# A token mixer rewritten as one software pipeline with a Toeplitz convolution and a list scheduler, on eight Trainium2 cores

## The chip, the cores and the metric

The kernel runs on the eight cores of one Trainium2 chip. Each core works alone on its own half of a stream, and no core talks to another. The metric is the device time of the slowest core in microseconds (us). Executions fall into two states: in the slow one, the cores of one die, sometimes of both, show a lower granted TensorE clock, and the time is longer (in one run of the kernel before, 3508.7 us with the cores of one die at a clock of 0.82, against 3098 us at 0.95). The profile and the trace are of one execution, on its slowest core.

Names used below: TensorE does matrix multiplications ("PE" in the profile, its weight loads "PEld"), VectorE is "DVE", ScalarE "ACT", GpSimd "POOL", SyncE "SP". GpSimd and SyncE issue nearly all DMAs here. PSUM is the memory that the matmuls write, which the kernel uses as eight banks; SBUF holds the other tiles. In the traces here each engine runs its instructions in the order in which the program gives them to it (run e4 shows what that can cost: one wait of 117.8 us). The transfers of one issuing engine keep their order too: of those whose landing the traces before tell (249 of GpSimd, 211 of SyncE), none landed before one that the same engine had issued earlier.

## The reference, cut to what matters

```python
x = x + 0.5 * swiglu_ffn(x, g_ff1, w_ff1_in, w_ff1_out)      # 1024 -> 2 x 2816 -> 1024
z = rms_norm(x, g_mix) @ w_in                                # 1792 columns: conv value, conv gate, q, k, v
u = cv * sigmoid(cg)
c_out = silu(layer_norm(depthwise_causal_conv31(u) + b_dw))  # 512 channels, 31 taps
q, k = rope(rms_norm(q)), rope(rms_norm(k))                  # 8 query heads, 2 key heads of 64
a_out = sink_attend(q, k, v)                                 # own chunk of 64 and the two before it
x = x + concat(c_out, a_out) @ w_out
x = x + 0.5 * swiglu_ffn(x, g_ff2, w_ff2_in, w_ff2_out)
```

A core has 4096 prompt tokens, 128 tokens of history (the halo) and 64 sample tokens. The weights of one SwiGLU are 16.9 MB (22 loads of 512 KB and 22 of 256 KB in the trace), and the program puts the tiles of each stage in the place of those of the stage before. So it has three phases: A (first SwiGLU), the mixer, and C (second SwiGLU). The residual goes through DRAM between phases (`x1`, `x2`).

## The kernel before

Before the change every engine gets its instructions in the order in which the Python program writes them. The mixer takes four tiles of 1024 tokens, one after the other, and in each tile the stages GLU, Q/K, V, conv with attention, output projection follow each other. The conv uses a diagonal weight matrix per tap: 31 matmuls for 128 channels and 256 tokens.

```python
def conv_chunk(sub, c):                 # 128 channels, N = 256 tokens
    yb = nxt("ab") % 2
    for t in range(31):
        O.mm(pb[yb][:, 0:N], DIAG[:, c, t, :], rhs_fn(c, t), t == 0, t == 30)
    ...
def mixer(t):                           # one tile of 1024 tokens
    for i in range(4): ...              # GLU: value and gate projections, sigmoid on ScalarE
    qk_run(chains)                      # Q/K projections, norm, rotation
    ...                                 # V projections
    conv_run(subs, att_tail)            # conv, layer norm; attention is woven in
    ...                                 # attention of the remaining groups
    for (r, n, m0) in ...:              # output projection
        O.dma("sync", "x1%d" % xi, x[0:n, :], d.x1[r:r + n, :], rk=[("x1", r)])
        ...
        O.dma("gpsimd", "x2%d" % xi, d.x2[r:r + n, :], x[0:n, :], wk=[("x2", r)])
...
A.run(loads(A))                         # 22 up-weights, then 22 down-weights, all on the GpSimd queue
mixer_phase(K, base)
Cc.run(loads(Cc))
```

## Time and profile before

The median was 3098.5 us (3096.4 to 3099.8). The trace gives this division on the slowest core (core 5):

| stretch (us) | what | length | TensorE busy |
|---|---|---|---|
| 0 to 1048 | first SwiGLU | 1048 | about 99% from 110 on |
| 1048 to 1128 | border to the mixer | 80 | 7 us |
| 1128 to 2062 | mixer | 934 | 753 us |
| 2062 to 2111 | border to the second SwiGLU | 49 | 4 us |
| 2111 to 3098 | second SwiGLU | 987 | 959 us |

These are the lines of the windows view of the kernel before. Each line has the stretch, its length, then the busy microseconds and the instruction count of PE, PEld, DVE, ACT and POOL, then the granted clock, the share of time in which the 16 DMA engines were busy, and GB/s.

```profile
40.00:110.00 70.00, 67.00 (x365) 34.75 (x363) 21.60 (x59) 18.09 (x31) 13.19 (x25) 1.00 1.04 192
110.00:1000.00 890.00, 881.85 (x5251) 493.61 (x5249) 335.24 (x1030) 225.19 (x388) 35.77 (x67) 0.99 0.19 65
...
1048.00:1128.00 80.00, 7.02 (x43) 5.10 (x43) 11.85 (x35) 5.76 (x8) 12.96 (x24) 0.52 0.72 140
1128.00:2062.00 934.00, 753.11 (x4625) 436.93 (x4624) 421.59 (x992) 463.03 (x1004) 20.34 (x38) 0.91 0.15 45
2062.00:2111.00 49.00, 3.83 (x29) 2.66 (x29) 11.53 (x43) 5.67 (x9) 9.59 (x19) 0.50 0.94 182
```

The SwiGLUs are full: 881.85 of 890 us. In the two borders TensorE does nearly nothing while the DMA engines are busy for 72% and 94% of the time, and in the mixer TensorE is idle for 181 us. The waits view of TensorE in the mixer (microseconds in total, times, longest one) says what ends that idle time:

```profile
PE PS L207 <- DVE B_t L207: 95.2, 64, 3.8
PE PS L207 <- ACT B_t L207: 80.7, 52, 5.0
```

These are 116 short waits for the two engines that finish Q, K, the sigmoid and the softmax: a stage waits for its own chain because no other stage is at hand. The longest piece of the first border is one transfer. In the chain of waits (start, length, what), the load of the sample keys, issued 4 us after the mixer's first weights, takes 35 us:

```profile
1062.07 0.55 SPq L237
1062.66 0.58 SPq L237
1063.35 35.45 DMA B_t<-ck
```

### The profile page before, as it was taken

Reading aid. Unit: us, or ns where it says so; the run is one execution under the profiler, and the core shown is the slowest. Engines: PE = TensorE matmul, PEld = TensorE weight load, DVE = VectorE, ACT = ScalarE, POOL = GpSimd, SP = SyncE. Lnnn points to the kernel's source line nnn. Section 1 sums busy time; section 2 is a strip of 40 time slices with the busy share of each in tenths; the row PEclk is TensorE's granted clock in tenths of the full one; section 3 lists DMA queues with packets and bytes.
Section 4 is the critical chain, followed back from the end, with each engine's and each line's share of the span. In section 5 each row is a group of like instructions: output and inputs, shape, how many; then the busy total and the mean of one; then the engine's idle time right before and its main releaser. Section 6 shows DMA issues by size and latency. Waiting matters only on the chain.

```text
span 3098.4 us, 45235 instructions; the slowest of 8 cores (3075.5 to 3098.4 us)
## 1 busy us (share of the span) xinstructions
PE 2723.2 (88%) x16155; PEld 1537.3 (50%) x16155; DVE 1096.3 (35%) x2948; ACT 915.0 (30%) x1797; POOL 133.7 (4%) x253
## 2 busy tenths in 40 slices
PE   4899999999999546978877887757899999999998
PEld 2455555555555223733633734524455555555554
DVE  3234443333343225344445344423222233332211
ACT  2122222222221114453455545622111122211210
POOL 2100000000000100000000000011000000000000
PEclk9999999999999767989989999887899999999999
DMA  9712111111111430112111130059410111111110
GB/s 199 138 60 72 72 72 48 52 62 62 65 59 52 102 67 7 42 35 70 48 68 42 35 116 1 1 146 193 109 51 32 55 55 55 62 62 62 48 42 21
DMA packets 66731, 204.71 MB, mean 66 GB/s; under 512 B 9452, under 2 KB 11514, under 8 KB 66511
## 3 DMA queue, kind: packets, MB, share of 16 engines
q0 software_dynamic: 33520, 103.14, 13.6%
q1 hardware_dynamic: 32991, 98.68, 10.0%
q8 instruction: 133, 2.18, 0.3%
q14 instruction: 87, 0.71, 0.1%
HBM read 183.67 MB, written 61.39 MB: 79 GB/s over the span
## 4 chain that ended last, share of the span: by engine, by line
PE 75%; DMA 12%; ACT 6%; DVE 3%; issue 3%; POOL 0%; SPq 0%; ACTq 0%; DVEq 0%; POOLq 0%
PE PS L207 75%; ACT B_t L207 6%; DVE B_t L207 3%; DMA C_wd<-wd 2%; DMA A_wu<-wu 2%; DMA C_wu<-wu 2%; DMA A_wd<-wd 2%; DMA B_t<-ck 2%; DMA B_t<-x 1%; DMA x<-B_t 1%; DMA B_t<-sconv 0%; DVE A_sm L207 0%; SPq L237 0%; DMA B_t<-cv 0%; ACTq L179 0%
## 5 line engine op out<-in xcount | busy, mean ns | idle before, releaser
L207 PE MATMUL PS<-B_t 128*128 128x256 bf16 (+5 forms) x4620 | 752.6, 323 | 175.1 <-DVE B_t L207 91.5
L207 PEld LDWEIGHTS PS<-B_t 128*128 128x128 bf16 (+1 forms) x4620 | 436.9, 103 | 490.2 <-issue 294.3
L207 PE MATMUL PS<-A_xnt,A_wu 128*128 128x384 bf16 (+1 forms) x3872 | 650.5, 329 | 3.0 <-DVE A_h L207 2.1
L207 PE MATMUL PS<-C_xnt,C_wu 128*128 128x384 bf16 (+1 forms) x3872 | 631.2, 325 | 6.3 <-DVE C_h L207 3.0
L207 PEld LDWEIGHTS PS<-A_xnt,A_wu 128*128 128x128 bf16 x3872 | 377.0, 98 | 258.9 <-issue 6.1
L207 PEld LDWEIGHTS PS<-C_xnt,C_wu 128*128 128x128 bf16 x3872 | 378.6, 98 | 248.2 <-issue 8.3
L207 PE MATMUL PS<-A_wd,A_h 128*128 128x512 bf16 (+1 forms) x1496 | 330.3, 381 | 7.8 <-DMA A_wd<-wd 7.8
L207 PE MATMUL PS<-C_wd,C_h 128*128 128x512 bf16 (+1 forms) x1452 | 322.3, 383 | 13.2 <-DMA C_wd<-wd 13.2
L207 ACT ACTIVATE C_sa<-PS 128x384 f32<-128x384 f32 (+1 forms) x242 | 117.7, 486 | 721.6 <-PE PS L207 704.8
L207 ACT ACTIVATE B_t<-B_t 128x256 f32<-128x256 f32 (+5 forms) x467 | 235.2, 505 | 131.5 <-DVE B_t L207 92.9
L207 DVE TENSOR_TENSOR C_h<-PS,C_sa 128x384 bf16<-128x384 f32 (+1 forms) x242 | 131.8, 550 | 377.0 <-PE PS L207 376.9
L207 DVE TENSOR_TENSOR A_h<-PS,A_sa 128x384 bf16<-128x384 f32 (+1 forms) x242 | 133.9, 562 | 349.3 <-PE PS L207 349.2
L207 ACT ACTIVATE A_sa<-PS 128x384 f32<-128x384 f32 (+1 forms) x242 | 120.0, 496 | 448.2 <-PE PS L207 432.7
L207 PEld LDWEIGHTS PS<-A_wd,A_h 128*128 128x128 bf16 (+1 forms) x1496 | 146.6, 98 | 183.4 <-issue 13.3
L207 PEld LDWEIGHTS PS<-C_wd,C_h 128*128 128x128 bf16 (+1 forms) x1452 | 143.3, 99 | 189.2 <-issue 23.3
L207 ACT ACTIVATE B_t<-PS 128x512 bf16<-128x512 f32 (+5 forms) x252 | 122.0, 534 | 260.6 <-PE PS L207 260.6
L207 DVE TENSOR_TENSOR B_t<-PS,B_t 128x512 f32<-128x512 f32 (+6 forms) x194 | 120.2, 632 | 212.9 <-ACT B_t L207 131.8
L207 ACT ACTIVATE B_t<-PS,B_t 128x128 f32<-128x128 f32 (+4 forms) x288 | 127.3, 488 | 113.6 <-PE PS L207 109.3
L207 DVE SCALAR_TENSOR_TENSOR C_xr<-PS,C_xr 128x512 f32<-128x512 f32 (+1 forms) x66 | 45.6, 692 | 289.6 <-PE PS L207 289.6
L207 DVE TENSOR_TENSOR B_t<-B_t 128x256 f32<-128x256 f32 (+7 forms) x192 | 100.7, 525 | 53.4 <-ACT B_t L207 45.0
L207 DVE SCALAR_TENSOR_TENSOR A_xr<-PS,A_xr 128x512 f32<-128x512 f32 (+1 forms) x68 | 46.8, 689 | 186.7 <-PE PS L207 186.7
L207 DVE CAST B_t<-B_t 128x256 bf16<-128x256 f32 (+2 forms) x73 | 21.0, 291 | 206.5 <-ACT B_t L207 155.1
(52 smaller groups left out, 1022.3 us busy)
## 6 DMA issues: line engine op xcount, KB each, us to landing
A_xa<-xin SPq DMA_DIRECT2D x33, 512.0 KB, 3.7
A_xr<-xin SPq DMA_DIRECT2D x33, 512.0 KB, 5.6
x<-A_xr POOLq DMA_DIRECT2D x33, 512.0 KB, 3.3
B_t<-x SPq DMA_DIRECT2D x32, 512.0 KB, 6.6
x<-B_t POOLq DMA_DIRECT2D x32, 512.0 KB, 4.0
C_xa<-x SPq DMA_DIRECT2D x32, 512.0 KB, 5.1
C_xr<-x SPq DMA_DIRECT2D x32, 512.0 KB, 7.4
yout<-C_xr POOLq DMA_DIRECT2D x32, 512.0 KB, 2.9
```

The costliest lines, as they stand in the source:

```text
L207: self.P.add(eng, lambda e: getattr(e, meth)(**kw), r, w)
```

## The change

The intent is to keep TensorE busy in the mixer, and to give it less to do there. It has four parts.

1. **Toeplitz conv.** Tokens are permuted so that four phases (token number mod 4) of 32 channels fill 128 partitions. A weight matrix of 128 x 128 then holds four taps for four input and four output phases, and 9 matmuls replace 31: for 128 tokens and 512 channels, 4,608 columns in place of 15,872.
2. **One pipeline** over 32 groups of 128 tokens. Step n projects group n, attends for group n-1, convolves one eighth of a 1024-token tile (from step 10 on), and projects the output of group n-22. There are 10 steps of fill and 12 of drain. Conv inputs and outputs change layout through DRAM (`ud`, `zd`).
3. **A list scheduler** sets the order on every engine, in all three phases. It walks through the operations with a table of modelled costs, and looks ahead by up to 24 units (an operation, or a group of matmuls) on each engine.
4. **Conv weights** of 4.7 MB are made by VectorE in phase A and stored to DRAM, between the up-weights and the down-weights of the first SwiGLU.

Scores and values also use tiles of 64 rows or 64 columns in place of zero-padded full ones. The diff, cut to its core:

```diff
+WINDOW = {"sync": 24, "scalar": 24, "vector": 24, "gpsimd": 24, "tensor": 24}
+    def schedule(self):
+        ...                                   # per engine: first ready unit within WINDOW, else the one ready soonest
+        self.order = [o for u in order for o in units[u]]
-        for t in range(31):
-            O.mm(pb[yb][:, 0:N], DIAG[:, c, t, :], rhs_fn(c, t), t == 0, t == 30)
+        p = self.pb[6][:, half * 256:half * 256 + 256]
+        with self.O.group():
+            for dd in range(9):
+                O.mm(p, self.wr[q][:, half, dd * 128:(dd + 1) * 128], self.US[:, g, dd:dd + N], ..., dd == 8, loose=True)
+    def transp(self, QN, n, dst, q=True):
+        p = self.pb[6][:, 0:5 * n // 2].bitcast(BF16).rearrange("p (j n) -> p j n", j=5)
+        ...                                   # five transposes on TensorE
+        O.cp(dst[:, j0:5, :], p[:, j0:5, :])
+    def run(self, on_step=None):
+        for n in range(last_step):
+            if proj: self.glu_pe(n); self.glu_act(n)
+            if att: self.transp(trq, 128, self.QKT[n % 4])
+            ...                               # statistics, conv, scores, Q/K/V projections, values
+            if og >= 0:
+                for h in range(2):
+                    self.out_pe(r, 128, self.out_lhs(og), h)
-    A.run(loads(A))
-    mixer_phase(K, base)
+    def prologue():
+        step = conv_weights(K, A.wd_off + 15 * 2048)
+        for j in range(NJ):
+            A.load_w(j)
+        for g in range(16):
+            step(g)                           # VectorE makes the weights of 32 channels, GpSimd stores them
+        for j in range(NJ):
+            A.load_d(j)
+    A.run(prologue)
+    M = Mixer(K, base); M.setup(); M.run()
     Cc.run(loads(Cc))
+    P.schedule()
```

## The prediction

> **What bounds the kernel now.** The windows view splits the slowest core's 3098 us into three. First SwiGLU, to 1048 us: after a start of about 40 us TensorE is 99% busy (882 of 890 us between 110 and 1000). Mixer, 1048 to 2062: TensorE is busy 760 of 1014 us. Second SwiGLU, first up-projection at 2111: again 98 to 99%. The chain of waits shows what the rest is: 80 us between 1048 and 1128 (loads of ck and sconv behind 35 us of weights), then in each 1024-token tile about 31 us GLU, 34 us Q/K (TensorE 23 busy, waiting for ScalarE and VectorE), 127 us conv and attention (101 busy), 24 us output projection (x1 loads and x2 stores on the chain); the first tile takes 286 us, not 216. Last, 49 us (2062 to 2111) of waiting for the second SwiGLU's weights and x, and 13 us for its down-weights. Only the mixer and its borders can be won.
>
> **What the change does.** Both SwiGLUs keep their matmuls. In the mixer the 31-tap diagonal conv (31 matmuls of 256 columns per 128 channels and 256 tokens) becomes 9 matmuls for 4 tokens x 32 channels: 15,872 columns per 128 tokens become 4,608. At the trace's spacing of 0.111 us that is 4.9 us per group, 157 us in all. The other matmuls keep their columns. From the spacings 0.218/0.164/0.111/0.058 us (512/384/256/128 columns) the new mixer's matmuls sum to 500 us, against about 660 before (estimates). Costed with the durations of the same shapes, VectorE sums to 400 us (435 busy before), ScalarE to 320 (470): every step but those with a layer-norm tail stays TensorE-bound. Scores and values now use 64-row and 64-column tiles[...].
>
> **New costs.** 16 computed conv weights (4.7 MB) are stored between the first SwiGLU's weights, where the DMAs already show a share of 1: down-weights come later, +15 us. Conv inputs and outputs go through DRAM in runs of 256 to 528 bytes, and conv weights are read again for every tile (19 MB). Pipeline fill (10 steps) and drain (12) use engines badly; in the drain x1 loads, x2 stores, transposed conv outputs and the next weights share one in-order queue: about 60 us lost, most of it in the last 8 groups.
>
> **Sum (estimates).** First SwiGLU to 1063; border 5 (weights go into its up-weights' space while its last down-projection runs); mixer 640 (TensorE 500, so 78% dense); border 22 (most weights loaded in the drain; x, norm and transposes remain); second SwiGLU 967. Total 2697, say 2690 us, 8 in 10 between 2590 and 2820. Chances: faster by over 2% 0.97, within 2% 0.02, slower 0.01.
>
> **Would show it right:** mixer of 600 to 690 us, TensorE its busiest engine; idle of TensorE at the first border under 15 us, at the second under 35; conv matmuls near 576 x 0.111 = 64 us; first SwiGLU 10 to 20 us longer; second unchanged.
>
> **Would make it wrong:** small-run DMAs saturating the queues (DMA share near 1 in the middle of the mixer); the scheduler's static order, made from modelled costs, stalling in-order engines; head-of-line waits on the GpSimd queue in the drain over 100 us[...].

The sum: 1063 + 5 + 640 + 22 + 967 = 2697 us. The spacings are close to the medians in the trace of the kernel before: 0.216, 0.163, 0.109 and 0.056 us for 512, 384, 256 and 128 columns.

## More of the kernel before

The start is needed for comparison later. The timeline of TensorE in the kernel before shows its longest wait between matmuls there (in brackets: idle time and what ended it), and the first up-projection at 41 us:

```profile
35.41 1.01 PE L207 MATMUL PS<-K_t,A_xb 128*128 128x128 bf16 x8 [11.11 <-DVE A_sm L207]
...
41.19 14.04 PE L207 MATMUL PS<-A_xnt,A_wu 128*128 128x448 bf16 x64 [0.94 <-ACT A_xnt L207]
```

## The result and the profile after

The changed kernel is correct and takes 2823.4 us (median of 4 runs, 2819.4 to 2860.8) against 3099.1 us in the same rounds. The ratio is 0.914, with a 95% interval of 0.906 to 0.922. Ratios in this document are the mean time of one kernel's fast runs over that of the other's in the same rounds, so not quite the ratio of the medians quoted. One of the four runs (2860.8 us) counts as fast although two of its cores had a clock of 0.935 and the others 0.955. Without it the mean is 2822.1 us, and that is the figure with which the experiments are compared.

The direction was right and the time was just outside the range, 3 us above its upper end and 133 us above the predicted 2690. By stage (slowest core, core 1, span 2817.9 us):

| stage | before | predicted | after | after minus predicted |
|---|---|---|---|---|
| first SwiGLU ends at | 1048 | 1063 | 1091 | +28 |
| border to the mixer | 80 | 5 | 0 | -5 |
| mixer | 934 | 640 | 737 | +97 |
| border to the second SwiGLU | 49 | 22 | 30 | +8 |
| second SwiGLU | 987 | 967 | 960 | -7 |

These are the lines of the windows view of the kernel after, with the same columns as before. The mixer is cut at its first conv (1246), its first steps with everything in them (1435), and its last conv (1667).

```profile
40.00:110.00 70.00, 22.91 (x120) 12.01 (x121) 17.29 (x57) 8.96 (x16) 12.10 (x23) 0.84 1.04 190
...
1091.00:1246.00 155.00, 122.62 (x761) 58.60 (x757) 72.21 (x202) 73.26 (x133) 9.69 (x16) 0.86 0.26 60
1246.00:1435.00 189.00, 146.04 (x950) 75.05 (x950) 97.80 (x205) 100.98 (x168) 21.06 (x43) 0.90 0.33 89
1435.00:1600.00 165.00, 153.29 (x954) 78.05 (x954) 96.22 (x203) 84.58 (x143) 19.87 (x34) 0.96 0.46 136
...
1670.00:1740.00 70.00, 30.16 (x129) 12.46 (x126) 32.18 (x62) 14.73 (x18) 23.92 (x42) 0.77 0.74 199
1740.00:1828.00 88.00, 34.56 (x127) 13.93 (x128) 11.68 (x19) 0.00 (x0) 14.96 (x29) 0.66 0.90 191
1828.00:1858.00 30.00, 3.20 (x28) 2.13 (x27) 11.28 (x48) 7.01 (x11) 7.40 (x14) 0.55 1.02 207
```

Three places are worth reading.

**The start.** Between 40 and 110 us TensorE was busy for 67.00 us before and for 22.91 after. The timeline of TensorE in the kernel after shows two long waits, both for the row statistics (`A_sm`) that VectorE makes, but for two reasons:

```profile
57.84 1.01 PE L343 MATMUL PS<-K_t,A_xb 128*128 128x128 bf16 x8 [36.06 <-DVE A_sm L343]
...
62.10 20.52 PE L343 MATMUL PS<-A_xnt,A_wu 128*128 128x448 bf16 x96 [0.94 <-ACT A_xnt L343]
109.19 1.01 PE L343 MATMUL PS<-K_t,A_xb 128*128 128x128 bf16 x8 [26.58 <-DVE A_sm L343]
```

The first wait (36.06 us) comes from the load of the third tile of x: ScalarE, which sums its squares, waits for it, and VectorE waits for ScalarE. The timeline of ScalarE:

```profile
51.08 1.06 ACT L343 ACTIVATE A_xb<-A_xa 128x1024 bf16<-128x1024 f32 x1 [28.17 <-DMA A_xa<-xin]
```

The conv weights are not its cause: it is there in e1 (33.3 us), which makes none at the start, and in e5 (28.5 us), which has none at all. What held VectorE before the second wait (26.58 us) is in its own timeline:

```profile
103.37 2.63 DVE L343 TENSOR_TENSOR W_wb<-W_ey,W_co 128x1152 bf16<-128x1152 f32 x2 [27.64 <-DMA wdc<-W_wb]
```

Here a conv weight (`W_wb`) waits for its buffer, that is, for the store of the conv weight two before it. The store shares the GpSimd queue and the DMA engines (share 1.04) with the up-weights. VectorE runs in order, so the row statistics stand behind the conv weight.

**The middle of the mixer.** From 1246 to 1435 TensorE is busy 146 of 189 us, from 1435 to 1600, where steps also have an output projection, 153 of 165. The waits view of TensorE from 1091 to 1600:

```profile
PE PS L343 <- DVE B_qn L343: 28.9, 15, 4.0
PE PS L343 <- DVE B_qkt L343: 21.4, 17, 7.0
PE PS L343 <- ACT B_pt L343: 9.8, 13, 1.5
```

`B_qn` is the normalised query and key, which the transposes read; `B_qkt` is the copy of the transposes out of PSUM. The waits cost more than their own length here. After such a wait the nine conv matmuls of a step take 2.08 us (the line at 1357.73, shown with e13), and without one, in the same trace:

```profile
1459.31 1.15 PE L343 MATMUL PS<-B_us,B_wr 128*128 128x256 bf16 x9
```

The granted clock was 0.90 from 1246 to 1435, where TensorE was idle for 43 of 189 us, and 0.96 from 1435 to 1600, where it was idle for 12 of 165. An estimate from the starts of all matmuls in the trace, each shape at its usual spacing (0.216 us for 512 columns, 0.109 for 256), divides the mixer's 737 us into 471 us of matmuls at that spacing, 198 us of idle time, and 68 us in which matmuls follow each other more slowly. Up to the last conv these are 416, 105 and 58 us.

**The drain.** After the last conv, 16 groups still need their output projection, 256 matmuls of 0.218 us or 56 us. They take 158 us (1670 to 1828). The chain of waits of the kernel after shows where the time goes, here six of its pieces from 1720 on:

```profile
1720.37 13.73 DMA C_wu<-wu
...
1736.39 25.41 DMA B_mt_161<-zd
1761.89 0.44 DVE B_mc_145 L343
...
1762.46 5.13 PE PS L343 x14
...
1767.69 0.70 DVE B_x_128 L343
...
1768.94 26.77 DMA x<-B_x_128
```

The weights of the second SwiGLU (`C_wu`) are being loaded by then. A conv output (`B_mt_161`) and an `x2` store each take some 26 us to land. Earlier in the mixer, 24 loads of conv outputs (into `B_mt_160`) landed in 3.8 us (median; 2.6 to 10.0).

Border 2 shrank from 49 to 30 us; the first border is gone, because the mixer's weights land while the last down-projection runs.

### The profile page after: what moved, and what is told of

It reads as the page before. It is cut to its first block, busy times and chain, and to the rows that moved or that the text cites. A ratio compares the mean times of both kernels' runs of the same rounds, so it can differ in the third digit from the quotient of the medians.

```text
span 2817.9 us, 41303 instructions; the slowest of 8 cores (2803.6 to 2817.9 us)
## 1 busy us (share of the span) xinstructions
PE 2492.3 (88%) x14740; PEld 1365.4 (48%) x14740; DVE 1032.1 (37%) x2701; ACT 747.9 (27%) x1303; POOL 216.3 (8%) x380
## 4 chain that ended last, share of the span: by engine, by line
PE 81%; DMA 9%; DVE 4%; issue 3%; ACT 2%; POOL 0%; SPq 0%; DVEq 0%; POOLq 0%; ACTq 0%
PE PS L343 81%; DMA wdc<-W_wb 3%; DMA x<-B_x_128 1%; DMA W_ey<-eye 1%; DMA B_mt_161<-zd 1%; DMA B_mt_160<-zd 1%; DVE B_y L343 1%; DMA C_wu<-wu 0%; ACT B_pt L343 0%; DMA B_x_128<-x 0%; DMA C_xa<-x 0%; DVE W_wb L343 0%; DMA B_hc<-sconv 0%; DVE B_qn L343 0%; ACT B_sq L343 0%
## 5 line engine op out<-in xcount | busy, mean ns | idle before, releaser
L343 PE MATMUL PS<-C_wd,C_h 128*128 128x512 bf16 (+1 forms) x1452 | 315.3, 379 | 0.0
L343 PE MATMUL PS<-B_xn,B_wi 128*128 128x512 bf16 x512 | 126.5, 398 | 8.5 <-DVE B_t_76 L343 3.4
L343 PE MATMUL PS<-K_t,A_xb 128*128 128x128 bf16 (+1 forms) x544 | 42.9, 224 | 84.1 <-DVE A_sm L343 62.6
L343 PE MATMUL PS<-B_us,B_wr 128*128 128x256 bf16 (+1 forms) x576 | 88.2, 309 | 30.2 <-DVE B_qkt L343 17.6
L343 PE MATMUL PS<-B_wi,B_xn 128*128 128x256 bf16 (+1 forms) x512 | 92.6, 335 | 8.3 <-ACT B_pt L343 8.3
L343 PE MATMUL PS<-B_wo,B_mc_145 128*128 128x512 bf16 x64 | 20.7, 453 | 83.0 <-DVE B_mc_145 L343 51.0
L343 ACT ACTIVATE A_xb<-A_xr 128x1024 bf16<-128x1024 f32 (+1 forms) x34 | 35.8, 1053 | 201.5 <-DVE A_xr L343 201.5
L387 POOL DMA_DIRECT2D yout<-C_xr x33 | 17.6, 535 | 928.2 <-DVE C_xr L343 928.2
L343 ACT ACTIVATE B_pt<-PS 128x1024 bf16<-128x1024 f32 (+1 forms) x68 | 66.1, 984 | 78.6 <-PE PS L343 78.6
```

The source lines that it names most:

```text
L343: o = self.P.add(eng, lambda e: getattr(e, meth)(**kw), r, w, cost=self.cost(eng, meth, kw))
L387: self.P.add(eng, lambda e: e.dma_start(out=out, in_=in_), r, w, lane=lane, rk=rk, wk=wk, cost=1.0 if eng == "gpsimd" else 0.5, nbytes=n * ...
```

## The experiments

All runs but e5 start from the changed kernel, and all of them gave correct results. Times are the mean of the fast runs (2 to 4 of them); "-" means faster than the changed kernel at 2822 us. The runs come from several rounds, between which the mean of the kernel before moved by 4 us (3096 to 3100), so a difference of 4 or 5 us between rows of different rounds says nothing.

| run | edit | us | against 2822 | ratio to before |
|---|---|---|---|---|
| e1 | conv weights made later | 2787 | -35 | 0.900 |
| e2 | mixer's DMAs on the SyncE queue | 2814 | -9 | 0.908 |
| e3 | second SwiGLU's weights after the last `x2` row | 2796 | -26 | 0.903 |
| e4 | no scheduler | 3123 | +301 | 1.008 |
| e5 | scheduler on the old mixer | 2875 | +53 | 0.927 |
| e6 | conv with 31 matmuls | 2940 | +118 | 0.948 |
| e7 | scheduler's costs from the trace | 2818 | -4 | 0.909 |
| e8 | first 8 up-weights early, rest late | 2813 | -9 | 0.907 |
| e9 | e1 and e3 together, down-weights last | 2757 | -65 | 0.891 |
| e10 | e9, weights 6 groups earlier | 2762 | -60 | 0.892 |
| e11 | e9 and e7 | 2768 | -54 | 0.894 |
| e12 | look-ahead of 96 | 2830 | +8 | 0.914 |
| e13 | transposes in another PSUM bank | 2787 | -35 | 0.900 |
| e14 | e9 and e13 | 2726 | -96 | 0.880 |
| e15 | e14 and e12 | 2725 | -97 | 0.880 |

### What pays: the scheduler, the pipeline or the conv (e4, e5, e6)

e4 takes the scheduler away and lets every engine run in program order.

```diff
-    P.schedule()
```

> The changed kernel with each engine's instructions left in program order: no list scheduler. Theory A (the software pipeline, written so in the program, and the cheaper conv bring the gain; the scheduler refines): 2850 to 3000 us, still faster than before. Rival B (the order set by the scheduler brings the gain): 3050 us or more, no faster than before. Mostly it should be the fill and the middle of the mixer and its first border that lose.

It took 3123 us, 0.8% more than the kernel before. The waits view of its TensorE over the whole span begins like this:

```profile
PE PS L343 <- DVE A_sm L343: 127.9, 2, 117.8
PE PS L343 <- DVE B_x L343: 84.7, 31, 11.8
PE PS L343 <- DVE B_qn L343: 69.3, 18, 16.8
PE PS L343 <- DVE B_qkt L343: 59.2, 29, 24.9
```

In program order all 16 conv weights stand ahead of the first row statistics on VectorE (one wait of 117.8 us), and the mixer waits for each result in turn; it takes 936 us, as the old one did (934). The pipeline and the cheaper conv alone gain nothing in the mixer; what the borders gain is lost at the start, where the first SwiGLU ends at 1134 in place of 1048.

e5 is the reverse: the old kernel, its mixer and its diagonal conv, under the new scheduler. Only the matmul loops are marked as groups that must stay together.

```diff
-        for t in range(31):
-            O.mm(pb[yb][:, 0:N], DIAG[:, c, t, :], rhs_fn(c, t), t == 0, t == 30)
+        with O.group():
+            for t in range(31):
+                O.mm(pb[yb][:, 0:N], DIAG[:, c, t, :], rhs_fn(c, t), t == 0, t == 30)
...
+    P.schedule()
```

> The old kernel, with its tile-by-tile mixer and 31-matmul conv, ordered by the list scheduler of the changed kernel: the scheduler alone. Theory A (scheduler and pipeline need each other: the old mixer's stages share buffers, so little can move): the mixer takes 850 us or more in place of 934; with both borders shortened (weights load early) the whole is 2930 to 3050 us. Rival B (the order is what wins, whatever the mixer): 2880 us or less.

It took 2875 us. So the scheduler alone brings 225 of the 277 us: the old mixer goes from 934 to 802 us, with TensorE busy for 714 of them, and the first border from 80 to about 11 us. The old program's Q/K chains, V projections and conv were independent all along; only their order kept them apart.

e6 keeps the new pipeline but gives its conv the old number of columns, with 22 more matmuls per group on a weight of zeros (so the result stays right).

```diff
-            for dd in range(9):
-                O.mm(..., dd == 8, loose=True)
+            for dd in range(9):
+                O.mm(..., False, loose=True)
+            for dd in range(22):
+                O.mm(p, self.ZERO[:, :], self.US[:, g, dd % 9:dd % 9 + N], False, dd == 21, loose=True)
```

> The changed kernel with 22 more matmuls by a zero tile in each conv group: as many conv columns as the old conv (31 x 256), the same result. The extra 22 x 0.111 us x 64 groups are 156 us of TensorE time. Theory A (the middle of the mixer is bound by TensorE): the whole grows by 110 to 160 us, to 2930 to 2990. Rival B (the middle is bound by latencies between engines): it grows by less than 70 us.

It took 2940 us. The added matmuls are 22 x 64 x 0.111 = 156 us of TensorE, and 118 of them show: about three quarters of each microsecond that is added to TensorE in the steps with conv. With as many conv columns as the old conv, the new mixer is 65 us slower than the old one under the same scheduler (2940 against 2875). So it is worth having only with the shorter conv. (e6 still makes and stores the new conv's weights and moves its data through DRAM, which a pipeline with the old conv would not need; such a kernel was not run.)

### The start (e1)

e1 makes the conv weights in halves beside blocks 2 and later of the first SwiGLU, in a buffer above its tiles. Nothing of them stands before the first row statistics, or between the up-weights and the down-weights.

```diff
     def prologue():
-        step = conv_weights(K, A.wd_off + 15 * 2048)
         for j in range(NJ):
             A.load_w(j)
-        for g in range(16):
-            step(g)
+    A.extra = conv_weights(K, A.end)        # a generator; each up-projection from block 2 on takes one step of it
```

> The 16 conv weights are computed and stored in halves beside the third and later blocks of the first SwiGLU, in a buffer of their own, not between its first weights. Theory A (VectorE, in order, stands behind conv-weight buffers whose stores queue behind the first SwiGLU's weights; PE waits of 36 and 27 us follow from that): the first SwiGLU ends near 1050 in place of 1091 us, the whole is about 40 us shorter (2780), the mixer the same within 10 us. Rival B (the start is limited by the bytes on the DMA queues, 4.7 MB of 21 MB): the end moves by less than 25 us.

It took 2787 us, 35 less. The mixer starts at 1057 in place of 1091, and takes as long as before (1057 to 1794). The whole gain is in the start. TensorE's timeline in e1 has the first long wait still, and the second no more:

```profile
54.16 1.01 PE L343 MATMUL PS<-K_t,A_xb 128*128 128x128 bf16 x8 [33.26 <-DVE A_sm L343]
...
58.42 24.59 PE L343 MATMUL PS<-A_xnt,A_wu 128*128 128x448 bf16 x120 [0.94 <-ACT A_xnt L343]
```

So theory A holds for the second wait only. The 34 us by which the first SwiGLU ends earlier are the 27 us of the second wait, 5 us of waits for down-weights and some 4 us of the first, less a new wait of 1.4 us. The rest of the first wait comes with the scheduler's order of the loads: the old kernel under the scheduler (e5) starts its first up-projection at 54 us, the old kernel alone at 41. Which load is in the way was not tested.

### The drain (e2, e3, e8, e9, e10)

Two theories: the drain's transfers wait for each other in the GpSimd queue, whatever else is there; or they wait because the next weights fill the queue and the DMA engines. (The expectation of e2 speaks of weight loads of 1 MB; in the trace they are of 512 and 256 KB.) e2 moves the mixer's `x1`, `x2`, `zd` and `zs` transfers to the SyncE queue.

```diff
-        self.O.dma("gpsimd", "bx1%d" % i, self.X1[i][0:n, :], self.d.x1[r:r + n, :], rk=[("x1", r)])
+        self.O.dma("sync", "bx1%d" % i, self.X1[i][0:n, :], self.d.x1[r:r + n, :], rk=[("x1", r)])
```

> The mixer's x1 loads, x2 stores and conv-output stores and loads go from the GpSimd queue to the SyncE queue; only weights stay on the GpSimd queue. Theory A (in the drain, small transfers stand in the same in-order queue behind 1 MB weight loads; 20 to 27 us to land in place of 3 to 6): the stretch from the last conv matmul to the last output matmul falls from 160 to 100 us or less, the whole by 40 to 70 us (2750 to 2780). Rival B (the DMA engines have no time left: share 0.9 in that stretch): the drain stays within 20 us of 160, or what it gains is lost again at the border to the second SwiGLU.

It gained 9 us. The drain after the last conv fell to 101 us, but the last conv itself ended at 1717 in place of 1667. With nothing else before them in the GpSimd queue, the second SwiGLU's weights began to load at 1597, not at 1715, and met the last convs: from 1600 to 1640 the DMA share was 1.03, TensorE waited up to 14.1 us for conv weights, and an `x2` store took 41.9 us to land. SyncE's queue had waits of its own (55.3 us between 1600 and 1860 for `x2` rows that VectorE had still to finish). So the collision moved to an earlier place. The drain that took 101 us had fewer weights beside it, and this run does not say whether the queue or the DMA engines were what it waited for. The store of 41.9 us was in SyncE's queue and the weights in GpSimd's: in this run a queue of its own did not keep a transfer from landing late beside them.

e3 leaves the transfers where they are and holds all weights of the second SwiGLU back until the last `x2` row is stored.

```diff
-        self.O.dma("gpsimd", self.tag + "wu%d" % (j % 8), self.WU[:, j, :], self.wu[j])
+        self.O.dma("gpsimd", self.tag + "wu%d" % (j % 8), self.WU[:, j, :], self.wu[j], rk=self.wait)
...
+    Cc.wait = [("x2", 31 * 128)]
```

> The second SwiGLU's weights wait until the mixer's last x2 rows are stored. Theory A (the weights in the queue delay the drain): the drain falls from 160 us to about 90 us, but the border to the second SwiGLU grows from 30 to 50 us or more, with waits for down-weights after it; in total within 30 us of the change, either way. Rival C (the drain is bound by its own chain of layer norm, store, transposed load, copy and x1/x2 round trips on three buffers): the drain stays above 130 us without any weight load beside it, and the whole becomes slower by 20 to 40 us.

It took 2796 us. The windows view of this run, drain and second SwiGLU:

```profile
1670.00:1763.00 93.00, 62.59 (x262) 25.84 (x260) 43.78 (x81) 16.20 (x21) 24.01 (x42) 0.85 0.61 197
...
1790.00:2793.00 1003.00, 962.32 (x5563) 539.71 (x5561) 268.96 (x698) 178.30 (x333) 31.56 (x60) 0.98 0.24 64
```

The drain took 93 us in place of 158. Its conv outputs landed in 3.1 us and its `x2` stores in 4.1 (medians). So 65 us of the drain are contention with the weights, shown by taking the weights away; how much of it is the shared queue and how much the DMA engines stays open. But the second SwiGLU took 1003 in place of 960: from 1790 to 1950 TensorE waits there 17.7 us for up-weights and 10.6 us for the normalised inputs. The net gain is 26 us. What the contention costs is also what the prefetch earns, in part.

e8 lets the first 8 up-weights go out early and holds back the rest, in the hope of both.

```diff
+    def early(n):
+        if n == 33:
+            for j in range(8):
+                Cc.load_w(j)
...
+        Cc.wait = [("x2", 31 * 128)]        # for the other 14 and all down-weights
```

> Eight of the second SwiGLU's 22 up-weights are loaded as soon as the projections are done, before the drain; the other weights wait for the mixer's last x2 rows. Theory A (weights beside the drain delay it, but weights all after it delay the next stage): the drain is about as short as without weights (95 us in place of 160) and the second SwiGLU does not start more than 30 us after it nor grow by more than 15 us: 2755 to 2780 us. Rival B (any saved wait comes back as DMA time): 2795 us or more, as with all weights afterwards.

It took 2813 us, a miss. The eight weights went out by 1605, before the last convs: TensorE waited 8.1 us for conv weights (3.0 in the changed kernel), the last conv ended at 1687, 20 us later, and the second SwiGLU still took 988 us. e9 joins e1 and e3, and lets the down-weights go only after the up-weights.

```diff
+    A.extra = conv_weights(K, A.end)
+    Cc.wait = [("x2", 31 * 128)]
-        self.O.dma("gpsimd", self.tag + "wd%d" % (j % 8), self.WD[:, j, :], self.wd[j])
+        self.O.dma("gpsimd", self.tag + "wd%d" % (j % 8), self.WD[:, j, :], self.wd[j], rk=[(self.tag + "wu", NJ - 1)] if self.wait else ())
```

> Two mends in one: conv weights built later in the first SwiGLU (as in the first experiment, 36 us), and the second SwiGLU's up-weights only after the mixer's last x2 rows, its down-weights only after its up-weights (in the third experiment down-weights shared the queue and the first block then grew by 42 us). If the start and the drain's contention are separate losses they add: 2740 us (2725 to 2760), the drain 95 us, the second SwiGLU's span at most 985 us. If rival: gains do not add, 2770 or more.

It took 2757 us: the gains of e1 (35) and e3 (26) add, since they lie in different stages. The third edit did not do its part: the second SwiGLU took 1000 us, where at most 985 were expected. e10 releases the weights at the 26th group of `x2` rows in place of the last.

```diff
-    Cc.wait = [("x2", 31 * 128)]
+    Cc.wait = [("x2", 25 * 128)]
```

> As the run before, but the up-weights are let go when the 26th of 32 row groups is stored, so that they load beside the last six output groups. If DMA time beside the drain is free for the taking: 10 to 20 us faster than the run before. If they again stand ahead of x1 loads and x2 stores in the queue: no faster, the last output 15 us or more later.

It took 2762 us. The last output projection came 38 us later than in e9, and the second SwiGLU was 38 us shorter. Six groups of lead moved the loss from one stage to the next and gained nothing.

### The middle of the mixer (e7, e11, e12, e13, e14, e15)

Four theories for the 55 us that the fill and the middle took beyond the prediction: the scheduler's cost table is wrong, its look-ahead is too short, a shared PSUM bank forbids the better order, or the chain of dependences itself is too long. e7 sets the costs from the trace (in that of the changed kernel ScalarE takes 490 ns for 384 columns and 1022 for 1024, VectorE 680 for 512 and 783 for 608, and the DMA engines move up to 424 KB per us, in slices of 1 us).

```diff
-                pipe = max(pipe, end + 0.5) + units[u][0].nbytes / 230e3
+                pipe = max(pipe, end + 0.5) + units[u][0].nbytes / 370e3
-                lat = 0.06 if eng[x] == e else 0.16
+                lat = (0.0 if e == "tensor" else 0.1) if eng[x] == e else (0.28 if e == "tensor" else 0.12)
...                                          # and the fixed parts of each engine's cost
```

> The scheduler's cost table is set to durations and spacings read from the traces (ScalarE 0.175 us + n/1200, VectorE 0.09 + n/960, small matmuls not below 0.058, transfers at 370 in place of 230 KB per us, longer latency after TensorE); the program is the same. Theory A (the idle of the fill and the middle of the mixer comes from orders made with wrong costs): the mixer up to its last conv matmul, 576 us, falls by 25 us or more. Rival B (dependences and buffers set it): within 15 us.

It took 2818 us, 4 less. The mixer's first matmul to its last conv took 566 us in place of 576, but the drain lost most of that: the table hardly matters. With the edits of e9 (run e11, which is those two diffs together) it was even 10 us slower than e9, because the first SwiGLU then ended at 1066 in place of 1051.

> The run with both mends, ordered with the calibrated cost table. Alone that table was worth 6 us, the time to the last conv matmul 9 us less. Expected: 5 to 15 us faster than with both mends and the old table; a difference below 5 us would say that the costs hardly matter.

That run missed its expectation; why the new costs lengthen the first SwiGLU was not looked into. e12 widens the look-ahead.

```diff
-WINDOW = {"sync": 24, "scalar": 24, "vector": 24, "gpsimd": 24, "tensor": 24}
+WINDOW = {"sync": 24, "scalar": 96, "vector": 96, "gpsimd": 24, "tensor": 96}
```

> The changed kernel with the scheduler's look-ahead on TensorE, VectorE and ScalarE widened from 24 to 96 instructions or groups. Theory A (look-ahead limits the overlap in the fill and the middle of the mixer): the 576 us from the mixer's first matmul to its last conv matmul fall by 20 us or more. Rival B (dependences, PSUM banks and buffers limit it, and in the fill there is nothing else to run): within 10 us.

It took 2830 us: the mixer's first matmul to its last conv took 585 us in place of 576. With the longer look-ahead the scheduler found no better order. The timeline of TensorE in the changed kernel shows one such step:

```profile
1352.35 0.27 PE L343 MATMUL PS<-B_y_152,B_e_134 128*128 128x256 bf16 x1
1356.22 0.44 PE L343 MATMUL PS<-K_t,B_qn 128*128 128x128 bf16 x5 [3.60 <-DVE B_qn L343]
1357.73 2.08 PE L343 MATMUL PS<-B_us,B_wr 128*128 128x256 bf16 x9 [1.07 <-DVE B_qkt L343]
```

TensorE idles 3.60 us until the normalised queries are there, transposes them, idles another 1.07 us until VectorE has copied the transposes out, and then runs a conv that needs neither. The conv (`B_us`, `B_wr`) comes after because transposes and conv write PSUM bank 6, and the program counts a bank as one buffer: in program order the transposes come first, so the conv has to wait for the copy, and no scheduler may move it ahead. The scores that follow need the copy anyway, and they use bank 2. That bank held the projection from which the transposes' input was made, so it is free by then. So e13 writes the transposes into bank 2.

```diff
     def transp(self, QN, n, dst, q=True):
-        p = self.pb[6][:, 0:5 * n // 2].bitcast(BF16).rearrange("p (j n) -> p j n", j=5)
+        p = self.pb[2][:, 0:5 * n // 2].bitcast(BF16).rearrange("p (j n) -> p j n", j=5)
```

> The changed kernel with one edit: the query and key transposes write PSUM bank 2 (whose projection they wait for anyway) in place of bank 6, which they share with the conv. Theory A, the shared bank forbids TensorE to run a conv while it waits for the normalised queries: TensorE's waits for B_qn and B_qkt between 1091 and 1600 us fall from about 50 us to under 20, the mixer's first matmul to its last conv takes 540 to 560 us in place of 576, total 2790 to 2808. Rival B, the chain from projection to transposes is itself what the step waits for: the waits move to other lines, under 8 us gained, total 2815 to 2830.

It took 2787 us, 35 less for one digit. First matmul to last conv took 546 us in place of 576. The next line is the group of the conv matmuls in the changed kernel (count, busy, mean ns, then TensorE's idle time before them), and the one after it the same group in this run:

```profile
L343 PE MATMUL PS<-B_us,B_wr 128*128 128x256 bf16 (+1 forms) x576 | 88.2, 309 | 30.2 <-DVE B_qkt L343 17.6 <-ACT B_y L343 8.7 <-DMA B_wr<-wdc 3.0
```

```profile
L343 PE MATMUL PS<-B_us,B_wr 128*128 128x256 bf16 (+1 forms) x576 | 81.7, 293 | 15.7 <-ACT B_y L343 10.4 <-DMA B_wr<-wdc 3.6 <-DVE B_ma L343 1.7
```

The wait of the conv for `B_qkt` (17.6 us) is gone. The total of the two waits, for `B_qn` and `B_qkt`, fell only from 50.3 to 36.6 us (28.9 to 25.2, and 21.4 to 11.4), not to under 20 as expected of this theory; the time fell by slightly more than it said (2790 to 2808). The estimate from the matmuls' starts shows why the time fell by more than these waits: up to the last conv idle time fell from 105 to 86 us, and the time of slower matmuls from 58 to 44. This run puts 35 us on the bank that transposes and conv shared.

e14 and e15 add the edit to e9, and e15 the longer look-ahead too (the diffs are those shown).

> The fastest version so far (late conv weights and weights after the last x2 row, 2755 to 2759 us) with the transposes in bank 2. Theory A: 2725 to 2745. Rival B: 2750 to 2765.

> The same with a look-ahead of 96 operations on TensorE, VectorE and ScalarE. If the bank was what kept the larger look-ahead from helping (it gained nothing before): 5 to 15 us faster than the run with bank 2 alone. If not: within 5 us of it.

They took 2726 and 2725 us. The bank's 32 us add to the rest. The look-ahead stays worth nothing, so the bank was not what had kept it from helping. At 2725 us this is the fastest version, 12% faster than the kernel before and 3.4% faster than the changed one.

## Why the prediction was right or wrong

**Right: what bounded the kernel, the direction, and the untouched stages.** Only the mixer and its borders could be won, and were: the second SwiGLU took 960 us where 967 were predicted. TensorE stayed the busiest engine in the mixer (539 us of the 737). The first border came out under 15 us (0), and the second under 35 (30). The mean clock did not fall: it was 0.952 on the slowest core, against 0.943 to 0.949 before. (In the mixer alone it was 0.86, from 1091 to 1828, against 0.91 before, from 1128 to 2062. It was 0.91 from 1091 to 1600, and 0.71 in the drain, where TensorE was busy for 65 of 158 us.) The small-run DMAs did not saturate the queues in the middle of the mixer: the DMA share was 0.39 from 1246 to 1600.

**Wrong, the step that failed first: "mixer 640 (TensorE 500, so 78% dense)".** It measured 737. The TensorE sum of about 500 us was not what failed: the matmuls at their usual spacings in the trace come to 493 us if none overlap (an estimate), or 471 with the overlap that was measured. The density was: 493 of 737 us is 67%, where 78% was predicted and the old mixer had 70% (657 of 934, counted in the same way). The sum had no term for matmuls that follow each other more slowly after waits, 68 us here; the conv's matmuls, expected near 64 us, were busy for 88. And two of its terms were mis-sized:

- *"about 60 us lost, most of it in the last 8 groups"*: the drain took 158 us for 56 us of matmuls, a loss of 102. The cause named, the drain's transfers beside the next weights in one in-order queue, is right as to the weights: e3 shows that 65 us of the loss are contention with them. That the queue itself is what they contend for is not shown. The prediction listed head-of-line waits over 100 us among what would make it wrong, but gave them no weight in the sum.
- *Fill and middle*: what was left of the predicted 640 (640 - 56 - 60 = 524 us) measured 579, 55 more. The claim that *"every step but those with a layer-norm tail stays TensorE-bound"* compared the busy sums of engines per step, and a sum cannot see a wait within a step. e13 shows that 30 us of it come from one PSUM bank shared by transposes and conv. e7 and e12 show that the fear of *"the scheduler's static order, made from modelled costs"* was unfounded as to costs and look-ahead. Some 25 us remain. TensorE's waits for the normalised queries (25.2 us in e13) are of that size, and the slower matmuls (44 us there) are another candidate; no run tells them apart.

**Wrong: "down-weights come later, +15 us".** The start lost 43 us, and TensorE's waits for down-weights were only 5.0 us of it (7.8 in the kernel before). What cost was the row statistics: 26.6 us because VectorE stood in order behind a store of conv weights, which e1 gives back, and a first wait that grew from 11.1 to 36.1 us because a tile of x landed late, which comes with the scheduled order of the loads (e5 has it without any conv weights). The prediction put the conv weights on the DMA engines' account only, and had no term for the new order of the loads.

**Slightly off: the second border,** predicted 22, measured 30. The DMA share there is 1.02.

**Not counted:** what the 64-row and 64-column tiles save. The sum had no term for it, and the trace shows a little. These are the first value matmuls of a group in the timeline of TensorE in the changed kernel (start, length, shape, count):

```profile
1125.25 0.30 PE L343 MATMUL PS<-B_pt,B_v 128*64 128x256 bf16 x2
1125.38 0.28 PE L343 MATMUL PS<-B_pt,B_one 128*64 128x256 bf16 x2
1125.59 0.30 PE L343 MATMUL PS<-B_pt,B_v 64*64 64x256 bf16 x2
1125.72 0.27 PE L343 MATMUL PS<-B_pt,B_one 64*64 64x256 bf16 x2
1125.92 0.30 PE L343 MATMUL PS<-B_pt,B_v 128*64 128x256 bf16 x2
```

Eight matmuls start in 0.67 us (1125.25 to 1125.92), 0.084 us each where a full one of 256 columns has 0.109: nearly a quarter less. Two 512-column score matmuls take 0.32 us (from the start of a pair to that of the next matmul, the median of 46 pairs with no wait after them), where two full ones take 2 x 0.216. By these rates the tiles saved about 20 us (an estimate, from the tiles' count and these spacings).

**Not seen at all: what does the work.** The prediction credited the pipeline and the conv. e4 and e5 show that the order is worth more: without the scheduler the new mixer gains nothing, and the scheduler alone takes the old kernel to 2875. The part of the new mixer, given the scheduler, is the remaining 53 us, and e6 shows that it rests on the shorter conv.

**What stays open:** the remaining 25 us of fill and middle; which load makes the first tile of the start wait; whether the drain's transfers contend for the queue or for the DMA engines; why the calibrated costs lengthen the first SwiGLU (e11); and how to have both a drain without contention and a second SwiGLU that finds its weights there. e10 shows that the moment of release alone does not do it.

## What to carry to other kernels

When an in-order engine waits, ask which independent work stands behind the wait, and what keeps it there: program order (a list scheduler gained 225 us on unchanged code), a shared PSUM bank (35 us for one digit), or other transfers under way (65 us in the drain). A helper computation given to an "idle" engine cost here what its slowest dependence held up behind it (26.6 us at the start), not its busy time; and the prefetch beside busy transfers was paid for by the urgent ones that then landed later (conv outputs in 14 to 26 us, where others had landed in 3.8). Cost a pipeline's fill and drain as stages of their own, with the waits of their longest chain, and not by busy sums. And check with a run that removes the supposed cause that the wait really goes: of the two waits at the start that looked alike, only one did.
